# Rotated queries and keys stored to DRAM head by head instead of part by part

## The chip, the cores and the metric

The kernel runs on one core of one Trainium2 chip. The metric is device time in microseconds, here called us: the median over executions of the whole program, lower is better. A core has TensorE (PE, with its weight loads PEld), VectorE (DVE), ScalarE (ACT), GpSimd (POOL) and SyncE (SP). Each runs its own list of instructions in order. SyncE and GpSimd issue the DMA transfers, and sixteen transfer engines that they share carry them out.

## What is computed

The reference is one step of a two-layer decoder trunk for 1024 prompt tokens and 64 sample tokens that share weights. Layer 0 is attention with a window of 128 tokens, 16 query heads and 4 key heads of 64 dimensions; layer 1 is retention. The change lies in layer 0, where queries and keys are projected, rotated and used block by block:

```
q, k, v, g = split(h @ w_in)
q = rope(q);  k = rope(k)          # [x1*cos - x2*sin, x2*cos + x1*sin], two halves of 32
s = q @ k_band.T / 8               # 128 queries against this block's keys and the block's before
p = sink_softmax(s, sink, mask)
y = (p @ v_band * silu(g)) @ w_out
```

## The kernel before, in words

Tokens lie along the free dimension, 1088 of them in three chunks of 384, 384 and 320 (`CH`); the last 64 are the sample tokens. Every float32 product is made of three passes on values split into a high and a low part (`split`, L302 to L304: ScalarE writes the high part, VectorE the rest).

A projection of two weight slots is `pair_t` (its matmuls are L137 to L139). The columns of q and k are sorted so that the 128 partitions of a result are four heads of 32 rows, and the two results of a pair are the two halves of the rotary dimension. `attn_k` (L437) makes all four key heads at once; `attn_q` (L506) makes the four query heads of one key head `kv`, so there are four calls of it. For each chunk the evacuation scales and rotates the result on VectorE (`rope`), splits it into the tile `qk_hl` of shape [128 partitions = head and row, 2 = high or low, 2 = half, tokens], and stores it with four DMAs issued on GpSimd's queue: L448 for keys into `s_k`, L515 for queries into `s_q`. Each takes one part (high or low of one half), 128 partitions with one row of 384 tokens each, 1536 bytes (256 tokens, 1024 bytes, in the last chunk). In DRAM `s_k` is [head, part, 64 rows, token], and `s_q` is [kv, 128 rows = four parts of 32, head, token]. There are 12 stores of keys and 48 of queries. `qk_hl` has two buffers.

The attention itself is cut into units: for each of four `kv` eight blocks of 128 prompt tokens and two groups of sample tokens. `attn_load` (L548) issues a unit's loads on SyncE's queue: `qst` from `s_q` (L552), two copies of `kwin` from `s_k` (L557, 64 partitions each) and `vst` (L559). `attn_scores` multiplies them (L594, L595); softmax, transposes (`attn_turn`, L631, L654 to L658) and values (`attn_values`, L668, L682, L690) follow, and the gated result `og` goes to `s_og` by a store on GpSimd's queue (L693). `og` and `qst` have two buffers. Units run staggered and are woven into the stream of the remaining projections (`weave` in `layer0`): the matmuls of `L0_ORDER` (g0 q1 q2 g1 q3 g2 g3 and the two embedding projections p0 p1) give the beat, and steps of units are put between them at a fixed rate, once the chunk they need is in `self.done`. Weights come through SyncE's queue too (`wraw`, L109), as do the embeddings `praw` (L323), which are split into buffers of `qk_hl`.

The build plans each engine's order of instructions with a simulated time line (`schedule_with_timeline_sim=True`); which semaphore each waits for follows from what it reads and writes.

Of the kernel before, what the change touches and what calls it, by code (L numbers as in the profile page):

```python
# [9 lines left out]
F32 = mybir.dt.float32  # L10
# [45 lines left out]
class Trunk:  # L56
# [380 lines left out]
    def attn_k(self, pool, acts):  # L437
        nc = self.nc

        def evac(c, ps, c0, n):  # L440
            self.norm_rows(c)
            r = self.rope(pool, ps, n, c0)
            m = min(n, TP - c0)
            hl = pool.tile([P, 2, 2, 384], F32R, name="qk_hl")
            self.split(hl[:, 0, :, :m], hl[:, 1, :, :m], r[:, :, :m])
            for ab in range(2):
                for half in range(2):
                    nc.gpsimd.dma_start(self.s_k[:, ab, half * 32:half * 32 + 32, c0:c0 + m], hl[:, ab, half, :m].bitcast(F32))  # L448
            if c == 2:
                for half in range(2):  # L450
                    nc.gpsimd.dma_start(self.s_kn[half * 32:(half + 1) * 32, :, :].rearrange("r k t -> k r t"),
                                      r[:, half, 256:320])
                for lo, rows, dst in ((128, P, "p"), (256, TS, "s")):
                    pt = self.pa.tile([P, 512], F32, name="pa")
                    for half in range(2):
                        nc.tensor.transpose(pt[:rows, half * P:(half + 1) * P], r[:, half, lo:lo + rows], self.ident)
                    kn = pool.tile([P, 4, 2, 32], F32, name="knat" + dst, bufs=1)
                    nc.scalar.copy(kn[:rows], pt[:rows, 0:256].rearrange("p (h k r) -> p k h r", h=2, k=4))
                    flat = kn[:rows].rearrange("p k h r -> p (k h r)")
                    if dst == "p":  # L460
                        nc.gpsimd.dma_start(self.io["kwp"], flat)
                    else:
                        nc.gpsimd.dma_start(self.io["kws"][:, 120:128, :], flat)

        yield from self.pair_t(acts, evac)
# [40 lines left out]
    def attn_q(self, pool, acts, kv):  # L506
        nc = self.nc

        def evac_q(c, ps, c0, n):
            r = self.rope(pool, ps, n, c0)  # L510
            m = min(n, TP - c0)
            hl = pool.tile([P, 2, 2, 384], F32R, name="qk_hl")
            self.split(hl[:, 0, :, :m], hl[:, 1, :, :m], r[:, :, :m])
            for j in range(4):
                nc.gpsimd.dma_start(self.s_q[kv, j * 32:(j + 1) * 32, :, c0:c0 + m].rearrange("r h t -> h r t"),  # L515
                                  hl[:, j // 2, j % 2, :m].bitcast(F32))
            if c == 2:
                for half in range(2):
                    nc.gpsimd.dma_start(self.s_qs[kv, half * 32:(half + 1) * 32].rearrange("r h t -> h r t"),
                                      r[:, half, 256:320])  # L520
            self.done.add(("q", kv, c))

        yield from self.pair_t(acts, evac_q)
# [861 lines left out]
```

## Time and profile before

| what | us |
|---|---|
| median of 3 runs | 1669.41 |
| lowest and highest | 1668.7, 1670.39 |
| profiled execution, its own time | 1670.7 |
| its span, first to last instruction | 1668.9 |
| TensorE busy in the span | 1642.2 |
| mean granted TensorE clock | 0.997 |

The profile shows the one profiled execution; its times count from the span's start. Layer 0 with the changed stores takes the first quarter, to about 424 us. [...] A wait is put down to the releaser that came last by the profile.

### The profile page before, as it was taken

The page shows a single profiled execution, that of the slowest core. Times are in us where ns is not written, and L with a number is a line of the kernel's source. Part 1 is how long each engine was busy: PE and PEld are TensorE (multiplying, and loading weights), DVE is VectorE, ACT ScalarE, POOL GpSimd, SP SyncE. Part 2 cuts the span into 40 slices and gives each one's busy share as a digit, 9 for nine tenths or more (in the row PEclk, how much of TensorE's full clock was granted, in tenths as well). Part 3 has the DMA queues.
Part 4 walks back from the last instruction along what each step waited for, and adds up shares of the span by engine and source line. Part 5 has one row for each costly group of instructions (what it writes and reads, how often), then busy time and mean ns, then how long its engine had stood idle before and what let it go on. Part 6 is the DMA issues. An engine that isn't in the chain of part 4 may idle for free.

```text
span 1668.9 us, 26266 instructions
## 1 busy us (share of the span) xinstructions
PE 1642.2 (98%) x9656; PEld 1536.3 (92%) x9656; DVE 994.8 (60%) x1952; ACT 592.9 (36%) x1357; POOL 377.1 (23%) x610
## 2 busy tenths in 40 slices
PE   8999999999999999999999999999999999999998
PEld 7999898999999999799979998799978998999998
DVE  7569787977148585146734665456735765543952
ACT  6245454686334351222222312222222533231421
POOL 1515544345001121111122212131122221200000
PEclk9999999999999999999999999999999999999999
DMA  8655646586314443253545555365544766572342
GB/s 284 186 155 136 169 117 166 177 260 206 122 38 158 144 142 126 75 185 130 186 147 177 191 171 171 117 198 177 191 154 146 259 209 203 189 240 84 124 145 88
DMA packets 180175, 273.07 MB, mean 164 GB/s; under 512 B 30560, under 2 KB 129824, under 8 KB 180016
## 3 DMA queue, kind: packets, MB, share of 16 engines
q1 hardware_dynamic: 143216, 178.01, 34.8%
q0 software_dynamic: 36832, 93.40, 16.4%
q8 instruction: 76, 1.25, 0.3%
q14 instruction: 51, 0.42, 0.1%
HBM read 173.51 MB, written 99.68 MB: 164 GB/s over the span
## 4 chain that ended last, share of the span: by engine, by line
PE 71%; issue 2%; DMA 1%; POOL 0%; ACT 0%; DVE 0%; POOLq 0%; ACTq 0%; SPq 0%; DVEq 0%
PE pj L137 16%; PE pj L139 16%; PE pj L138 16%; PE pj L237 4%; PE pj L238 4%; PE pj L239 4%; PE pa L1109 1%; PE pa L1117 1%; PE pa L1042 1%; PE pa L984 1%; PE pa L1044 1%; PE pa L1043 1%; PE pa L953 1%; PE pa L1026 1%; PE pa L1025 1%
## 5 line engine op out<-in xcount | busy, mean ns | idle before, releaser
L137 PE MATMUL pj<-act,whi 128*128 128x384 f32 (+1 forms) x2160 | 711.7, 330 | 4.1 <-ACT ys L767 2.8
L139 PE MATMUL pj<-act,wlo 128*128 128x384 f32 (+1 forms) x2160 | 708.5, 328 | 0.0
L138 PE MATMUL pj<-act,whi 128*128 128x384 f32 (+1 forms) x2160 | 708.2, 328 | 0.0
L137 PEld LDWEIGHTS pj<-act,whi 128*128 128x128 f32 x2160 | 407.0, 188 | 10.2 <-ACT ys L767 3.1
L138 PEld LDWEIGHTS pj<-act,whi 128*128 128x128 f32 x2160 | 407.2, 189 | 3.2
L139 PEld LDWEIGHTS pj<-act,wlo 128*128 128x128 f32 x2160 | 406.9, 188 | 2.9 <-issue 0.8
L303 ACT CAST whi<-wraw 128x512 fp32r<-128x512 f32 (+1 forms) x226 | 128.0, 614 | 182.7 <-PE pj L138 130.0
L304 DVE TENSOR_TENSOR wlo<-wraw,whi 128x512 fp32r<-128x512 f32 (+1 forms) x226 | 146.3, 680 | 75.2 <-ACT whi L303 74.2
L237 PE MATMUL pj<-whi,act 128*128 128x512 f32 x256 | 102.4, 401 | 0.0
L238 PE MATMUL pj<-wlo,act 128*128 128x512 f32 x256 | 101.1, 395 | 0.0
L239 PE MATMUL pj<-whi,act 128*128 128x512 f32 x256 | 100.6, 394 | 0.0
L911 ACT ACTIVATE rp_a<-pj,rcol 128x512 f32<-128x512 f32 x32 | 22.0, 689 | 125.1 <-PE pj L239 97.6
L1119 DVE SCALAR_TENSOR_TENSOR s<-s,pa 128x512 f32<-128x512 f32 x64 | 42.7, 683 | 37.6 <-PE pa L1117 37.3
L352 DVE TENSOR_TENSOR rp_a<-pj,cs 128x768 f32<-128x768 f32 (+1 forms) x39 | 35.5, 911 | 49.4 <-PE pj L139 49.3
L542 ACT ACTIVATE s_sb<-s_sb,nm 128x129 f32<-128x129 f32 (+1 forms) x136 | 53.6, 397 | 30.8 <-DVE nm L539 30.5
L237 PEld LDWEIGHTS pj<-whi,act 128*128 128x128 f32 x256 | 48.1, 188 | 16.3 <-issue 3.4
L239 PEld LDWEIGHTS pj<-whi,act 128*128 128x128 f32 x256 | 48.1, 188 | 11.1
L238 PEld LDWEIGHTS pj<-wlo,act 128*128 128x128 f32 x256 | 48.1, 188 | 10.2
L1120 POOL DMA_DIRECT2D srs<-s x64 | 35.6, 557 | 92.8 <-DVE s L1119 90.7
L943 POOL TENSOR_TENSOR br<-bv,mhalf 128x1 f32<-128x1 f32 x36 | 29.5, 820 | 112.2 <-DVE bv L940 112.2
L840 DVE SCALAR_TENSOR_TENSOR ple_st<-ple_st,pleh 128x768 f32<-128x768 f32 (+2 forms) x25 | 22.0, 881 | 52.6 <-ACT ple_st L839 52.6
L364 ACT ACTIVATE rp_a<-rp_b 128x768 f32<-128x768 f32 (+1 forms) x36 | 29.2, 810 | 68.1 <-DVE rp_b L362 55.8
(252 smaller groups left out, 2580.9 us busy)
## 6 DMA issues: line engine op xcount, KB each, us to landing
wraw<-wt SPq DMA_DIRECT2D x110, 512.0 KB, 4.1
s<-st SPq DMA_DIRECT2D x16, 1024.0 KB, 6.5
srs<-s POOLq DMA_DIRECT2D x64, 256.0 KB, 2.9
act<-s_og SPq DMA_DIRECT2D x48, 192.0 KB, 3.7
qst<-s_q SPq DMA_DIRECT2D x32, 256.0 KB, 4.2
qk<-s_qk SPq DMA_DIRECT2D x32, 256.0 KB, 3.7
s_v<-rp_a POOLq DMA_DIRECT2D x32, 256.0 KB, 2.3
vl<-s_v SPq DMA_DIRECT2D x32, 256.0 KB, 2.8
```

The lines of the kernel that those rows point to most:

```text
L137: mm(ps, hi[:, sl], a[c][:, 0], start=start and i == 0, stop=False)
L138: mm(ps, hi[:, sl], a[c][:, 1], start=False, stop=False)
L139: mm(ps, lo[:, sl], a[c][:, 0], start=False, stop=stop and i == last)
L237: mm(o, hi, w[0][:, sl], start=first, stop=False)
L238: mm(o, hi, w[1][:, sl], start=False, stop=False)
L239: mm(o, lo, w[0][:, sl], start=False, stop=last)
L303: self.nc.scalar.copy(hi, x)
L304: self.nc.vector.tensor_tensor(out=lo, in0=x, in1=hi.bitcast(F32), op=ALU.subtract)
L352: nc.vector.tensor_tensor(out=ta, in0=ps, in1=self.cs[:, 0:1, c0:c0 + n].broadcast_to([P, 2, n]), op=ALU.mult)
L542: nc.scalar.activation(s[:, h, :], s[:, h, :], AF.Exp, bias=nm[:, h, :], scale=0.125, accum_out=den[:, h:h + 1])
L1119: nc.vector.scalar_tensor_tensor(out=s0, in0=s0, scalar=float(gam ** 8), in1=pd, op0=ALU.mult, op1=ALU.add)
L1120: nc.gpsimd.dma_start(self.io["srs"][4 * g + j, h, k * P:(k + 1) * P, :], s0)
```

## The change

The four stores of a chunk no longer take one part each for all heads. Each takes one head: 32 partitions, and from each of them all four parts, four rows of 384 tokens. On the DRAM side the same bytes go to the same places; the order of the dimensions in the access is now row, part, token, where it was head, row, token. The loads, the tiles and everything else stay.

```diff
@@ attn_k, evac
-            for ab in range(2):
-                for half in range(2):
-                    nc.gpsimd.dma_start(self.s_k[:, ab, half * 32:half * 32 + 32, c0:c0 + m], hl[:, ab, half, :m].bitcast(F32))
+            for k in range(4):
+                nc.gpsimd.dma_start(self.s_k[k, :, :, c0:c0 + m].rearrange("a (f r) t -> r (a f) t", f=2),
+                                    hl[k * 32:k * 32 + 32, :, :, :m].bitcast(F32).rearrange("r a f t -> r (a f) t"))
@@ attn_q, evac_q
-            for j in range(4):
-                nc.gpsimd.dma_start(self.s_q[kv, j * 32:(j + 1) * 32, :, c0:c0 + m].rearrange("r h t -> h r t"),
-                                  hl[:, j // 2, j % 2, :m].bitcast(F32))
+            for h in range(4):
+                nc.gpsimd.dma_start(self.s_q[kv, :, h, c0:c0 + m].rearrange("(j r) t -> r j t", j=4),
+                                    hl[h * 32:h * 32 + 32, :, :, :m].bitcast(F32).rearrange("r a f t -> r (a f) t"))
```

## Rows read from the trace of the kernel before

**Rows 1.** The page, busy us, share of the span and instructions of each engine.

```profile
PE 1642.2 (98%) x9656; PEld 1536.3 (92%) x9656; DVE 994.8 (60%) x1952; ACT 592.9 (36%) x1357; POOL 377.1 (23%) x610
```

**Rows 2.** What TensorE waited for: us in total, times, longest us.

```profile
PE pa L594 <- DMA wraw<-wt: 3.4, 1, 3.4
PE pa L682 <- ACT pts L658: 3.1, 1, 3.1
...
PE pa L668 <- ACT pth L303: 2.5, 1, 2.5
```

**Rows 3.** Stretches: length, busy us by engine, granted clock, DMA share, GB/s.

```profile
97.00:107.00 10.00, 6.63 (x32) 6.34 (x32) 4.15 (x8) 2.50 (x9) 0.10 (x1) 0.83 0.75 232
...
184.00:200.00 16.00, 12.91 (x83) 12.44 (x82) 9.57 (x22) 10.11 (x39) 5.44 (x8) 0.89 0.61 145
...
281.00:296.00 15.00, 12.50 (x72) 11.82 (x71) 9.02 (x18) 10.11 (x31) 1.09 (x4) 0.89 0.57 159
```

**Rows 4.** Time line of TensorE: start, us, instruction, idle before and releaser.

```profile
101.22 0.30 PE L594 MATMUL pa<-kwin,qst 128*128 128x128 f32 x1 [3.37 <-DMA wraw<-wt]
```

**Rows 5.** Time line of SyncE's queue: the first two loads of queries.

```profile
88.60 3.14 SPq L552 DMA_DIRECT2D qst<-s_q  x2
```

**Rows 6.** DMAs issued from 88 to 92 us: count, KB each, us to landing.

```profile
qst<-s_q SPq DMA_DIRECT2D x2, 256.0 KB, 12.2
...
s_q<-qk_hl POOLq DMA_DIRECT2D x2, 192.0 KB, 11.9
```

**Rows 7.** What SyncE's queue waited for, 74 to 92 us.

```profile
SPq L552 <- DMA s_q<-qk_hl: 13.7, 1, 13.7
```

**Rows 8.** Time line of GpSimd: stores of chunk 0 and chunk 1.

```profile
78.28 2.74 POOL L515 DMA_DIRECT2D s_q<-qk_hl  x4 [3.49 <-ACT qk_hl L303]
86.60 2.83 POOL L515 DMA_DIRECT2D s_q<-qk_hl  x4 [5.58 <-ACT qk_hl L303]
```

**Rows 9.** DMAs issued from 80.3 to 81 us, chunk 0's last stores.

```profile
s_q<-qk_hl POOLq DMA_DIRECT2D x2, 192.0 KB, 8.4
```

**Rows 10.** Time line of ScalarE before TensorE's second wait.

```profile
188.72 0.53 ACT L690 COPY og<-pa 64x32 f32<-64x32 f32 x4 [8.54 <-DMA s_og<-og]
```

**Rows 11.** DMAs issued from 178 to 178.7 us.

```profile
s_og<-og POOLq DMA_DIRECT2D x1, 128.0 KB, 10.6
```

**Rows 12.** All DMA issues of the span: count, KB each, median us to landing.

```profile
qst<-s_q SPq DMA_DIRECT2D x32, 256.0 KB, 4.2
...
kwin<-s_k SPq DMA_DIRECT2D x56, 128.0 KB, 4.3
s_q<-qk_hl POOLq DMA_DIRECT2D x32, 192.0 KB, 8.6
...
s_og<-og POOLq DMA_DIRECT2D x32, 128.0 KB, 3.4
...
s_x<-ys POOLq DMA_DIRECT2D x16, 192.0 KB, 2.8
...
s_v<-v_hl POOLq DMA_DIRECT2D x8, 256.0 KB, 3.8
...
praw<-pT SPq DMA_DIRECT2D x4, 384.0 KB, 5.4
```

**Rows 13.** Time line of ScalarE before TensorE's third wait.

```profile
283.14 0.83 ACT L303 CAST qk_hl<-praw 128x768 fp32r<-128x768 f32 x1 [4.18 <-DMA praw<-pT]
```

**Rows 14.** DMAs issued from 272 to 276 us.

```profile
praw<-pT SPq DMA_DIRECT2D x1, 384.0 KB, 7.6
```

**Rows 15.** Line 486, stores with four rows from each partition: ns min/median/max.

```profile
L486 POOL DMA_DIRECT2D s_v<-v_hl x8: 750/752/946, 35.0 to 46.1; - x8
```

**Rows 16.** Stretches of 2 us, columns as in rows 3.

```profile
80.00:82.00 2.00, 2.00 (x14) 2.00 (x13) 0.00 (x0) 0.00 (x0) 1.02 (x2) 1.00 0.28 44
...
84.00:86.00 2.00, 2.00 (x16) 2.00 (x15) 1.36 (x3) 0.53 (x1) 0.00 (x0) 1.00 0.47 120
...
100.00:102.00 2.00, 0.78 (x7) 0.81 (x8) 0.11 (x1) 0.00 (x0) 0.00 (x0) 1.00 0.98 354
```

## The prediction, made before the changed kernel ran

> **What bounds the kernel now.** I read the page's busy times first. TensorE is busy for 98% of the span [rows 1]: a change to stores can only win what TensorE idles, and what the lower clock after an idle stretch costs. So the second view is what TensorE waited for [rows 2]. Three of its waits lie in the attention stage, where the changed stores are: 3.4, 3.1 and 2.5 us. The third view shows the stretches around them [rows 3], and the reader is to see the granted clock beside the busy time: a mean of 0.83 over 10 us, 0.89 over 16 us and 0.89 over 15 us, while it is 1.00 elsewhere in the stage. [...] The lost time is (1 - clock) x stretch: 1.7, 1.8 and 1.65 us. One stop thus costs its wait and its clock: 3.37 + 1.7 = 5.1 us, 3.09 + 1.8 = 4.9 us, 2.5 + 1.65 = 4.15 us; 14.1 us together.
>
> Then I ask of each whether a changed store stands behind it.
>
> Stop 1. TensorE comes to the first scores of unit 0 at 101.22 - 3.37 = 97.85 us and starts them at 101.22 [rows 4]. The row names a weight load, but the matmul reads qst and kwin, and qst is what came last: SyncE issued its load at 88.60 [rows 5], and it took 12.2 us to land [rows 6], at 100.8. Why so late? SyncE had stood still for 13.7 us until the stores of s_q had landed [rows 7]; those four were issued from 78.28 at 0.69 us each [rows 8], and the last took 8.4 us to land [rows 9], so 80.3 + 8.4 = 88.7. And why 12.2 us for the load? It ran beside the next chunk's four stores, issued at 86.60 [rows 8], which themselves took up to 11.9 us [rows 6].
>
> Stop 2. TensorE waited for pts, which ScalarE wrote late because it stood for 8.5 us before og, until 188.7 [rows 10]: the buffer was still being stored. That store was issued on GpSimd's queue straight behind four stores of s_q and took 10.6 us to land [rows 11], against 3.4 us as a rule [rows 12].
>
> Stop 3. ScalarE stood 4.2 us for praw [rows 13], whose load took 7.6 us [rows 14]; four stores of s_q had been issued just before it.
>
> **The change, part by part.** Count and bytes stay: 48 stores of s_q and 12 of s_k, four to a chunk, 192 KB each [rows 12] and 128 in the last chunk by the code, every row still 1536 bytes (1024 in the last chunk). What changes is the shape of a store: 32 partitions with four rows each, instead of four groups (one per head) of 32 partitions with one row each, heads outermost.
>
> Issue on GpSimd: a store with four rows per partition is in the trace already, s_v: 0.75 us against 0.69 for s_q [rows 15]. 60 x 0.06 = 3.6 us more on GpSimd in the stage, 0.24 us per chunk, covered by GpSimd's idle time (it is busy 5.4 of the 16 us around stop 2, 1.1 of the 15 around stop 3 [rows 3]). If that cover were gone, the s_og store behind would start 0.24 us later, a tenth of the slack below. I put it at nothing.
>
> Landing: the changed store is not in the trace, so I bound it. Lower end: the fastest other stores of this size, s_x with 192 KB in 2.8 us [rows 12]. Upper end: no better, 8.4 us, or worse (rival 3). I take 3.8 us, from s_v [rows 12]: the row is nearest in what changes, partitions outermost and four rows apart within each, its rows 512 bytes in place of 1536 and its bytes more (256 KB); what it lacks is the narrowness, 128 partitions against 32. That the present form is slow for its shape and not for its bytes is what the fine windows say: with nearly only these stores in flight the transfer engines are busy to 0.28, at 44 GB/s, and later to 0.47, at 120, while a backlog a little later moves 354 GB/s at 0.98 [rows 16]. Most of the sixteen stand idle while everybody waits.
>
> [...]
>
> What then becomes of the stops. Stop 1: the last store of chunk 0 lands at 80.3 + 3.8 = 84.1 instead of 88.7. The qst load is issued 4.5 us earlier, before chunk 1's stores start at 86.6, and at its usual 4.2 us [rows 12] it lands at 88.3, 9 us before TensorE asks. Even a store of 7 us and a load of 8 us would do (80.3 + 7 + 8 = 95.3). The stop goes: 5.1 us. What is late next there is the load for unit 2, which needs unit 0's buffer; it follows unit 0's scores as before, only 3.4 us earlier, and TensorE does not wait for it now [rows 2].
>
> Stop 2: ScalarE went on to og, and then to pts, at 188.7; for TensorE not to wait the s_og store has to land 3.1 us earlier, in 7.5 us instead of 10.6. With the four stores ahead at 3.8 us it should need 3.4 to 5. It goes: 4.9 us. Stop 3: praw would have to land in 5.1 us instead of 7.6; its usual is 5.4 [rows 12], and a weight load competes too. It is open, and I count nothing for it.
>
> For s_k nothing is to be gained on TensorE: no wait of its own in [rows 2] lies where those loads are used first. A store by head also means that the first kwin loads need only the store of their own head; that too shortens a wait that costs nothing.
>
> Sum: 5.1 + 4.9 = 10.0 us off the profiled execution's 1670.7 us (span 1668.9), 1660.7. The median of the runs shown, 1669.41, is 1.3 below that execution, so the forecast is 1659.4 us.
>
> **The rivals.** (1) All three stops go. For it: the same stores stand beside the praw load. Against: 2.5 us are needed and the load's own median leaves 2.2. Time: 1669.4 - 14.1 = 1655.3.
>
> (2) The burst is bound by what the four stores move together, not by the form of each. 4 x 192 KB = 786 KB at the 120 GB/s of the best window with nearly only them in flight (84 to 86 us [rows 16]) take 6.6 us; with about 2.5 us of lead (at 80 to 82 us the rate is still 44 GB/s) they land at 87.4, 1.3 us sooner than now. Chunk 1 then still meets the qst load, and each stop shrinks by about 1 us: 1669.4 - 3 = 1666.4 at best and no change at worst. Against it: s_v stores of 256 KB follow each other closely too and land in 3.8.
>
> (3) Slower: the narrow source is the limit. Each store now draws on 32 partitions. If the last of a chunk then needs 12 us instead of 8.4, SyncE issues qst 3.6 us later, stop 1 grows by 3.6, and stop 2 by as much through the s_og store in the same queue: 1669.4 + 7.2 = 1676.6. It decides from the point where a chunk's last store needs more than 8.4 us. For it: kwin's loads to 64 partitions take 4.3 us for 128 KB where qst's to 128 take 4.2 for twice the bytes [rows 12]. Against: at 786 KB in 10 us the present rate is far under what the queues reach [rows 16].
>
> [...] No row of this trace shows a store of 32 partitions.
>
> (4) Part of the gain is taken back. The order of instructions on each engine is written by a planner at build time, from its own prices of transfers; other shapes may shift that order, and a new wait of 2 to 5 us with its clock may stand where TensorE runs ahead. One such stop leaves 1664 to 1668. The rows speak neither for nor against it.
>
> **How the numbers follow.** No change means within 0.2%, 3.3 us, about what a measurement of this kernel can tell. Forecast (stops 1 and 2 go, 3 stays or shrinks) 0.42; rival 1 0.20; rival 2 0.14; rival 3 0.10; rival 4 0.14. Faster: the forecast, rival 1 and most of rival 4, 0.72; no change: rival 2 and the rest of 4, 0.18; slower 0.10. The range runs from rival 1 with 1.3 us of small waits besides, 1654, to rival 2 at its worst, 1669.5; it leaves out rival 3 and a few per cent more. The forecast's own range is 1656 to 1663.
>
> **What would show it.** Right: s_q landing near 4 us instead of 8.6; SyncE's wait for s_q a few us instead of 13.7; no wait of TensorE before the first scores; granted clock 1.00 from 97 to 107 us; the s_og store behind a burst in about 4 us; ScalarE's wait before og gone. Rival 2 shows as first stores that land sooner and last ones that do not; rival 3 as landings above 8.4 us; rival 4 as a wait of TensorE at a line not in [rows 2]. The prediction is wrong if s_q lands in 4 us and the first stop stays: then qst was not what TensorE waited for.

## The result and the profile after

| | before | after |
|---|---|---|
| median, us | 1670.41 (6 runs, 1668.7 to 1676.4) | 1656.56 (6 runs, 1654.23 to 1658.56) |
| profiled execution, its own time | 1670.7 | 1655.34 |
| its span | 1668.9 | 1653.6 |
| mean granted clock | 0.997 | 0.999 |

The ratio is 0.9914, with a 95% interval of 0.9901 to 0.9927: faster by 0.9%, 13.9 us by the medians. The forecast was 1659.4, in a range of 1654.0 to 1669.5; it counted from a median before of 1669.41 (three runs), where six runs give 1670.41.

The page's busy line and what TensorE waited for in the kernel after, to be read beside [rows 1] and [rows 2]:

```profile
PE 1637.7 (99%) x9656; PEld 1532.7 (93%) x9656; DVE 995.0 (60%) x1952; ACT 593.8 (36%) x1357; POOL 371.8 (22%) x610
```

```profile
PE pa L196 <- ACT act L299: 5.0, 1, 5.0
PE pa L668 <- DVE pth L304: 1.4, 1, 1.4
PE pa L196 <- ACT whi L303: 1.1, 1, 1.1
```

The three stops of the attention stage are gone; the longest wait left, 5.0 us, lies at the program's start and was there before. A small one is new, 1.4 us at L668. The reader will miss a fourth line, which the prediction left out because it lies at the end of the layer. From what TensorE waited for in the kernel before:

```profile
PE pj L137 <- ACT ys L767: 2.8, 1, 2.8
```

The same three stretches as in [rows 3], shifted to where the work now stands, and one around the new wait (length, busy us by engine, granted clock, DMA share, GB/s):

```profile
94.00:104.00 10.00, 10.00 (x65) 10.00 (x64) 4.69 (x10) 3.45 (x12) 2.22 (x4) 1.00 0.51 145
...
180.00:196.00 16.00, 16.00 (x107) 15.44 (x106) 12.70 (x27) 10.41 (x39) 7.44 (x13) 1.00 0.82 221
...
276.00:292.00 16.00, 16.00 (x103) 15.59 (x102) 15.41 (x29) 10.40 (x26) 5.22 (x9) 1.00 0.60 178
...
360.00:370.00 10.00, 8.50 (x40) 7.25 (x39) 9.78 (x25) 6.52 (x23) 3.88 (x9) 0.83 0.65 218
```

TensorE is busy throughout the first three and the clock stays at 1.00; around the new wait the clock falls to 0.83. That gives an account of the 15.3 us between the two spans. Idle time of TensorE fell from 1668.9 - 1642.2 = 26.7 us to 1653.6 - 1637.7 = 15.9, by 10.8: the three stops 9.0, the wait for ys 2.8, less the new 1.4, and some tenths. Busy time fell by 4.5: the clock gave back 5.15 at the three stops and took 1.7 at the new wait, 3.45 net. Some 1 us has no row of its own. The profile's page gives the granted clock as a share of full speed: behind the first stop of the kernel before it reads 0.52 from 102 to 105 us, where matmuls of 384 columns start 0.32 us apart, and 1.00 from 108 to 111 us, where they start 0.17 to 0.18 us apart.

The DMA issues of the whole span, the answer to [rows 12]; then the first query loads in SyncE's time line and the stores in GpSimd's, for [rows 5] and [rows 8]:

```profile
qst<-s_q SPq DMA_DIRECT2D x32, 256.0 KB, 3.4
...
kwin<-s_k SPq DMA_DIRECT2D x56, 128.0 KB, 3.4
s_q<-qk_hl POOLq DMA_DIRECT2D x32, 192.0 KB, 3.8
...
s_og<-og POOLq DMA_DIRECT2D x32, 128.0 KB, 2.9
...
praw<-pT SPq DMA_DIRECT2D x4, 384.0 KB, 3.8
```

```profile
84.01 1.22 SPq L552 DMA_DIRECT2D qst<-s_q  x2
```

```profile
78.63 2.18 POOL L515 DMA_DIRECT2D s_q<-qk_hl  x4 [4.45 <-DVE qk_hl L304]
86.94 2.18 POOL L515 DMA_DIRECT2D s_q<-qk_hl  x4 [6.13 <-DVE qk_hl L304]
```

The 192 KB store lands in 3.8 us instead of 8.6, the loads beside it got quicker too, and qst is issued at 84.0 instead of 88.6.

### The profile page after: what moved, and what is told of

The parts are those of the page before. It is cut to its first block, busy times and chain, and to the rows that moved or that the text cites. A ratio compares the mean times of both kernels' runs of the same rounds, so it can differ in the third digit from the quotient of the medians.

```text
span 1653.6 us, 26261 instructions
## 1 busy us (share of the span) xinstructions
PE 1637.7 (99%) x9656; PEld 1532.7 (93%) x9656; DVE 995.0 (60%) x1952; ACT 593.8 (36%) x1357; POOL 371.8 (22%) x610
## 3 DMA queue, kind: packets, MB, share of 16 engines
q0 software_dynamic: 29792, 93.31, 15.7%
## 4 chain that ended last, share of the span: by engine, by line
PE 93%; DMA 2%; issue 2%; DVE 1%; ACT 1%; POOL 0%; SPq 0%; POOLq 0%; DVEq 0%; ACTq 0%
PE pj L137 22%; PE pj L139 22%; PE pj L138 22%; PE pj L237 4%; PE pj L238 4%; PE pj L239 4%; PE pa L1109 1%; PE pa L1117 1%; PE pa L1042 1%; PE pa L984 1%; PE pa L1044 1%; PE pa L1043 1%; PE pa L953 1%; PE pa L595 1%; PE pa L594 1%
## 5 line engine op out<-in xcount | busy, mean ns | idle before, releaser
L238 PEld LDWEIGHTS pj<-wlo,act 128*128 128x128 f32 x256 | 48.1, 188 | 10.2
L362 DVE TENSOR_TENSOR rp_b<-pj,rbc 128x768 f32<-128x768 f32 (+1 forms) x36 | 32.7, 909 | 34.8 <-PE pj L139 34.8
```

Of the source, the lines that this page charges most:

```text
L238: mm(o, hi, w[1][:, sl], start=False, stop=False)
```

## Experiments

A cause named in advance had to be told from others: that the landing of the query stores decides (my theory); that it is the planner's order of instructions, which did change (TensorE's list of instructions differs from the one before in several hundred places); that it is the keys; that it is not the outermost size but something else about the store. Every ratio below is to the kernel before, run on the same chip.

**e1: each kind of store alone.** Added to the changed kernel behind its last output, with a vector instruction that rewrites the tile between the steps, so that each waits for the one before; `d2` is [2, 65, 4, TP] and `d8` [8, 17, 4, TP], so that the outer dimension cannot be merged. After the five single stores come four by part, four by head, four wide, and the four small ones:

```diff
+part = lambda d, j: g(d[j * 32:(j + 1) * 32, :, 0:384].rearrange("r h t -> h r t"), x[:, j // 2, j % 2, :])
+head = lambda d, h: g(d[:, h, 0:384].rearrange("(j r) t -> r j t", j=4),
+                      x[h * 32:h * 32 + 32].rearrange("r a f t -> r (a f) t"))
+wide = lambda d, j: g(d[:, 0, 0:384], x[:, j // 2, j % 2, :])
...
+    for h in range(4):
+        g(ds[0:32, h, 0:384], x[h * 32:h * 32 + 32, 0, 0, :])
...
+             lambda: g(d2[:, 0:64, 0, 0:384], x[:, 0, 0, :]), lambda: g(d8[:, 0:16, 0, 0:384], x[:, 0, 0, :]),
```

> The changed kernel with a tail: after its last output is computed, stores of one tile go to scratch memory of their own, each kind alone with nothing else issued beside it. One store by part (four heads outermost), one by head (32 partitions, four rows each), one wide (the same 128 rows as by part, but as one dimension of 128), one with 2 and one with 8 outermost; then four by part, four by head, four wide, and four small ones (32 partitions, one row each). Spread theory (the outermost size decides): by part 5 to 6 us to landing, 2 outermost 7 or more, 8 outermost 3 to 4, wide and by head 2.3 to 2.8; the last of four by part about 8, of four by head and four wide 3 to 4; small 2 to 2.5. Packet theory (the 6 KB that lie together in a partition of the by-head store decide): wide, 2 and 8 outermost take the 5 to 6 us of by part, only by head is quick. Narrow theory (32 partitions cost something): by head is slower than wide by 0.5 us or more. The time of the whole grows by the tail, some 60 us, and says nothing.

DMA issues of the tail, one row from a window around each step (count, KB each, median us to landing); below them the last store of each burst of four 192 KB stores, from a window around that one:

```profile
d_part<-prb POOLq DMA_DIRECT2D x1, 192.0 KB, 5.4
d_head<-prb POOLq DMA_DIRECT2D x1, 192.0 KB, 2.6
d_wide<-prb POOLq DMA_DIRECT2D x1, 192.0 KB, 2.2
d_two<-prb POOLq DMA_DIRECT2D x1, 192.0 KB, 7.5
d_eight<-prb POOLq DMA_DIRECT2D x1, 192.0 KB, 3.7
...
d_small<-prb POOLq DMA_DIRECT2D x4, 48.0 KB, 1.8
...
d_part<-prb POOLq DMA_DIRECT2D x1, 192.0 KB, 8.2
d_head<-prb POOLq DMA_DIRECT2D x1, 192.0 KB, 3.7
d_wide<-prb POOLq DMA_DIRECT2D x1, 192.0 KB, 2.6
```

Two, four, eight and 128 outermost: 7.5, 5.4, 3.7, 2.2 us for the same rows of the same tile. The wide store has exactly the rows of the store by part and is the quickest of all, so neither the length of a row nor what lies together in a partition explains the slow form; the outermost size does. What passes between size and time stands in the packet records of e1's trace (start, length and size of each packet). All of a store's 196608 bytes go in 44 to 48 packets of 1536 to 4608 bytes. With 2, 4 and 8 outermost and wide, a packet of 4608 bytes takes about as long in each case, 178, 178, 178 and 196 ns in the median; what differs is how many of these packets move at once, and that number stands longest at 2, 4, 8 and 16. By head it stands longest at 16 too. Why the outermost size sets that number is not shown: the records do not name the engines.

The narrow theory holds in small: by head is 0.4 us slower than wide alone, just under the 0.5 us named in advance, and 1.1 us at the end of a burst. With as many packets in flight, one of 4608 bytes takes 361 ns in the median by head and 196 wide. What makes a packet slower by head is not shown. The price is far below the 3.6 us that rival 3 would have needed.

**e2 and e3: keys alone, queries alone.** e2 takes the first hunk of the change, e3 the second.

> Only the 12 stores of keys go by head, those of queries by part as before; the planner writes TensorE's order as in the kernel before. My theory (the query stores make the stops): ratio 1.000 to the kernel before, within 0.2%, the waits of 3.4, 3.1 and 2.5 us stay. Rival (the keys, which come first and free SyncE's queue, start the gain): faster by 5 us, 0.997, with the first stop gone.

> Only the 48 stores of queries go by head; every engine's order is that of the changed kernel. My theory: the whole gain, 0.991 to 0.993, no wait of TensorE over 1.5 us in the attention stage. Rival (the keys bring part of it): 0.994 to 0.997, with one of the stops back.

e2: ratio 0.9989 (0.9972 to 1.0005). What TensorE waited for in e2:

```profile
PE pa L682 <- ACT pts L658: 4.0, 1, 4.0
PE pa L594 <- DMA wraw<-wt: 3.3, 1, 3.3
PE pj L137 <- ACT ys L767: 2.8, 1, 2.8
```

The keys land in 4.2 us and SyncE waits only 3.9 us for the first of them, and still TensorE's first two stops stand. The third does not show in this execution, although the query stores were not changed: the load of praw landed in 5.3 us here and ScalarE waited 1.9 us for it. That stop was the least settled of the three. e3: ratio 0.9915 (0.9892 to 0.9938), the whole gain, with keys that land in 7.6 us (7.7 in the kernel before). The rival of the keys falls.

**e4: only the first query group by part again.**

```diff
+            if kv == 0:
+                for j in range(4):
+                    nc.gpsimd.dma_start(self.s_q[kv, j * 32:(j + 1) * 32, :, c0:c0 + m].rearrange("r h t -> h r t"),
+                                      hl[:, j // 2, j % 2, :m].bitcast(F32))
+            else:
...
```

> The changed kernel, with the stores of the first query group (kv 0) by part again. My theory: the first stop returns, 3.4 us before the first scores and some 1.7 us of clock, with qst again the load that comes last, and no other: 0.994 to 0.995 to the kernel before. Rival (the planner's other order took the stops away, whichever way the stores go): no wait before the first scores, 0.991 to 0.992.

Built this way the orders of TensorE, ScalarE, VectorE and SyncE are those of the changed kernel. The first scores in TensorE's time line, and two stretches around them:

```profile
101.56 0.30 PE L599 MATMUL pa<-kwin,qst 128*128 128x128 f32 x1 [3.45 <-DMA wraw<-wt]
```

```profile
98.00:104.00 6.00, 2.55 (x16) 2.48 (x16) 2.68 (x5) 0.84 (x1) 0.00 (x0) 0.93 0.73 240
104.00:110.00 6.00, 6.00 (x32) 6.00 (x31) 2.02 (x6) 2.59 (x11) 0.00 (x0) 0.79 0.34 98
```

(L599 is L594 of the kernel before.) The stop is back at 3.45 us, with a clock loss of 0.07 x 6 + 0.21 x 6 = 1.7 us; the qst load, issued at 88.4 beside the next burst, took 13.2 us to land, until 101.6, when TensorE starts. Nothing but twelve stores differs. The ratio, 0.9933 (0.991 to 0.9957), lies between what my theory and the rival expected and its interval holds both: the trace tells them apart, the ratio does not. In the profiled execution the wait at L668 brought no clock loss (its stretch stays at 1.00). One execution of the five took 1654.6 us, as little as the changed kernel's; what TensorE waited for in it is not recorded.

**e5: a third buffer for og in the kernel before.**

```diff
-        og = pool.tile([P, 2, P], F32, name="og", bufs=2)
+        og = pool.tile([P, 2, P], F32, name="og", bufs=3)
```

> The kernel before, all stores by part, with a third buffer for og; TensorE's and SyncE's orders are those of the kernel before. My theory of the second stop (ScalarE stands before og because its buffer is still being stored, behind a slow burst in GpSimd's queue): ScalarE's wait before og and TensorE's 3.1 us before L682 go, the first stop stays at 3.4; ratio 0.997, some 5 us. Rival (the values of that unit are late for another reason, its pts or loads): the wait at L682 stays at 2 us or more, ratio 0.999 to 1.001.

Ratio 0.9963 (0.9947 to 0.9978). What TensorE waited for:

```profile
PE pa L594 <- DMA kwin<-s_k: 5.0, 1, 5.0
PE pa L196 <- ACT act L299: 4.9, 1, 4.9
PE pj L137 <- ACT ys L767: 2.9, 1, 2.9
PE pa L668 <- ACT pth L303: 1.3, 1, 1.3
```

The wait at L682 is gone with stores by part and TensorE's old order: the second stop was the buffer of og, held by a store that landed late. The first stop stays (5.0 us here, put down to another load).

**e6 and e7: without the planner.** `schedule_with_timeline_sim=False` in the kernel before and in the changed one; TensorE's lists then differ in 60 lines only, but ScalarE's and VectorE's still differ in about 300 and 270.

> The kernel before without the planner: every engine takes its instructions in the order in which the program names them. Base for the next run. Both theories: the query stores land in 7 to 9 us, and some waits of TensorE in the attention stage are there; the time may be anywhere from 1660 to 1720.

> The changed kernel without the planner, so that its order differs from the run before in few places (60 lines of TensorE's 8,900) and the form of the stores is the difference. My theory: faster than the run before by what TensorE's waits on late query stores cost there, 5 to 15 us. Rival (the planner's order made the gain): the two within 3 us of each other.

e6: 1703.41 us, ratio 1.0182 (1.0152 to 1.0212), query stores of 192 KB land in 10.2 us. e7: 1692.31 us, 1.0120 (1.0098 to 1.0142), 3.7 us. The difference is 11.1 us of medians with nearly one order of TensorE. TensorE's waits in the attention stage differ most at the attention's values:

```profile
PE pa L668 <- ACT pth L303: 3.8, 1, 3.8
...
PE pa L668 <- DVE ptm L648: 2.5, 3, 1.6
...
PE pa L668 <- DVE og L674: 1.5, 1, 1.5
PE pa L594 <- DVE s_sb L602: 1.5, 1, 1.5
```

These are e6's; in e7 the first is 0.5, the second 1.7, and the last two are gone. The form by head is worth about as much in another order, at other waits; how much of the 11.1 us is due to the orders of ScalarE and VectorE is not separated.

**e8, e9, e10: stores by part on 128 partitions, made wide.** The scratch tensors are laid out so that the 128 rows of a store are one dimension; qst is loaded in two DMAs.

```diff
-        self.s_q = scratch("s_q", [4, P, 4, TP])
+        self.s_q = scratch("s_q", [4, 2, P, 2, TP])
+            for ab in range(2):
+                for half in range(2):
+                    nc.gpsimd.dma_start(self.s_q[kv, ab, :, half, c0:c0 + m], hl[:, ab, half, :m].bitcast(F32))
+            for a in range(2):
+                src = self.s_q[kv, a, :, :, n * P:(n + 1) * P].rearrange("(h r) f t -> (r f) h t", h=4)
+                nc.sync.dma_start(u["q"][a * 64:a * 64 + 64].bitcast(F32), src)
```

> All stores by part again, but the scratch tensors laid out so that the 128 rows of a store are one dimension of 128; queries are loaded by two DMAs of 64 partitions instead of one of 128. My theory: stores land in 2.3 to 2.8 us, a little sooner than by head, and the time is that of the changed kernel within 0.2% (0.990 to 0.993 to the kernel before), since no wait of TensorE is left for them to shorten. Rival (every us of landing counts): 0.988 or less. Rival (the form by part is itself at fault): landing above 5 us and 0.997 or more.

> The changed kernel once more, beside the wide one on the same chip, to tell 0.1% apart. Ratio 0.990 to 0.993 to the kernel before.

> The wide stores once more. My theory (a sooner landing is worth nothing where no wait of TensorE hangs on it): within 0.15% of the changed kernel in the run before. Rival (the 1.1 us that a burst lands sooner are worth something): 0.2% or more below it.

e8: 0.9898 (0.9876 to 0.9919), query stores of 192 KB in 2.8 us: by part is as quick as any once its outermost dimension is 128. Side by side on one chip, e9 (by head) has 1657.59 us, 0.9912 (0.9897 to 0.9926), and e10 (wide) 1654.13 us, 0.9895 (0.988 to 0.9911). The medians differ by 3.5 us, 0.21%, the ratios by 0.17%, and the intervals overlap; by the one the rival is met, by the other it is between the two, and it stays open. In e10 TensorE does not wait at L668, where e9 waits 1.4 us. Its order differs from the changed kernel's in many lines, so even a real gain would not be the landing's alone.

**e11 and e12: one group by part, in two orders.** e11 takes group 3 back to by part, e12 group 2, with the condition of e4.

> The changed kernel with the stores of the last query group (kv 3) by part. The planner then writes TensorE's order as in the kernel before but for 35 lines, while the stores of groups 0 to 2 go by head. My theory (late landings make the stops, in either order): the first stop and the one before L682 are gone; the third, behind a load of praw beside group 3's stores, may return with 1 to 2.5 us, and the wait of 2.8 us for ys at the end of the layer returns with the order; ratio 0.993 to 0.996. Rival (the order makes the stops): all of 3.4, 3.1 and 2.8 us are back, 0.998 to 1.001.

> The changed kernel with the stores of query group 2 by part, in the changed kernel's order but for 23 lines of TensorE's. My theory of the second stop: the s_og store behind that burst again takes 7 us or more to land, ScalarE again stands 4 us or more before og, TensorE 2 to 4 us before L682; the first scores do not wait; ratio 0.993 to 0.996. Rival (the second stop was bound to the old order): no wait at L682, 0.990 to 0.993.

e11: 0.9929 (0.9912 to 0.9946), at the edge of the 0.993 to 0.996 expected. TensorE's waits from 50 to 420 us, and the stretch of the first scores:

```profile
PE pj L137 <- ACT ys L767: 3.0, 1, 3.0
PE pj L137 <- ACT rp_a L342: 1.2, 1, 1.2
PE pa L668 <- ACT s_sb L601: 0.7, 1, 0.7
```

```profile
94.00:104.00 10.00, 10.00 (x65) 10.00 (x64) 4.67 (x10) 3.04 (x11) 2.64 (x5) 1.00 0.56 162
```

With nearly the old order the first two stops are gone because groups 0 to 2 land early, ScalarE waits 2.8 us for praw again, until 270.7, but TensorE only 0.7, at 281.0 (the 1.2 us lie at 357), and the wait for ys is back. The first two stops follow the landings; the wait for ys follows the order. The third stop follows ScalarE's wait for praw, run by run: 4.2, 3.4, 2.8 and 1.9 us in the kernel before, e5, e11 and e2, and TensorE's longest wait at L668 near it is 2.5, 1.3, 0.7 and none.

e12: 0.9908 (0.989 to 0.9926), no loss beside e9's 0.9912 on the same chip. The s_og store behind group 2's burst, and what ScalarE and TensorE did about it, from 150 to 200 us:

```profile
s_og<-og POOLq DMA_DIRECT2D x1, 128.0 KB, 9.4
```

```profile
ACT og L690 <- DMA s_og<-og: 5.9, 1, 5.9
```

```profile
PE pa L631 <- ACT og L690: 1.5, 1, 1.5
```

The mechanism returns as in [rows 10] and [rows 11], 9.4 us and 5.9 us, but TensorE loses only 1.5, without loss of clock over the 16 us around it. I had expected 2 to 4, before L682. I had also expected a ratio of 0.993 to 0.996; no wait at L682 and 0.990 to 0.993 is what the rival had named. So the late store and ScalarE's wait come back in this order, but the second stop at its full price shows only in the old one. Why the order lets so little of ScalarE's wait through is not shown.

## Why the prediction was right, point by point

*Stop 1.* Right in each link: store 3.8 us, as I had estimated from s_v's row (in e1 2.6 us alone and 3.7 as the last of four), qst issued at 84.0 (84.1 was forecast), no wait, clock 1.00. e4 shows the price: 3.45 + 1.7 us, in one order of instructions.

*Stop 2.* Right: s_og behind the burst lands in 4.8 us in the kernel after (3.4 to 5 was forecast), and ScalarE no longer waits there. e5 shows the link through og's buffer by itself. Its price of 4.9 us holds for the old order; in the new one, e12 shows 1.5 us for the same late store.

*Stop 3.* I counted nothing for it and gave its going 0.20 as rival 1. It went: praw's load behind the last burst lands in 3.7 us instead of 7.6. Its 4.15 us are a little more than the 3.9 us by which the measured gain, 13.9, exceeds the 10.0 forecast, and 1656.56 lies nearer to rival 1's 1655.3 than to 1659.4. What I mis-sized is the load: I took its usual 5.4 us [rows 12] as what remains. That median is of three loads that behave differently, 7.6 behind the burst, 3.5, and 5.4 some 90 us after the last query store, beside other stores; in the kernel after they take 3.7, 3.9 and 3.8. How far the load's time was the burst's doing is not shown by a run of its own.

*What was not in the sum.* The wait for ys, 2.8 us, which I left out as lying outside the stage, and the new wait at L668 with 1.4 us and up to 1.7 of clock. That they nearly cancel is luck. Both hang on the planner's order, which is rival 4's mechanism: the first stands also in e2, e5 and e11, in or near the old order, the second also in e3, e4, e9 and e12, in or near the new one. By terms, all read from the two profiled executions: 14.1 + 2.8 - 3.1 = 13.8, beside 15.3 between their spans; the 13.9 of the medians is another measure, and that it agrees so closely says little.

*Rival 2* (the burst is bound by what moves together): in e1 the last of four stores by head lands in 3.7 us against 2.6 for one alone, so four cost 1.1 us more, where the rival needed 87.4 - 80.3 = 7 us for the last. *Rival 3* (narrow): real, at 0.4 to 1.1 us.

*Issue on GpSimd.* Forecast 0.75 us, from s_v; it is 0.55, less than the 0.69 by part. Hidden either way.

*A sign read wrongly.* I wrote that SyncE would wait for s_q "a few us" instead of 13.7. It waits 10.2: it comes to that point at 73.8, while the stores are not issued until 78.6. My own figures, 13.7 - 4.5 = 9.2, said so.

## What to carry to other kernels

For a DMA like these stores, whose partition dimension has to be split into (outer, inner) on the DRAM side, look at the outer size first: with 2, 4, 8 and 128 the same 192 KB landed in 7.5, 5.4, 3.7 and 2.2 us. Choose the tile's cut or the scratch tensor's layout so that the outermost dimension is large: in the kernel, 32 by head landed in 3.8 us and 128 in e8 in 2.8, where 4 took 8.6. A store is worth hurrying only if something waits behind it (in e2 the keys landed in 4.2 us instead of 7.7, at a ratio of 0.9989): look for the buffer it holds, the load that reads it back, and the loads that run beside it. When a stop of TensorE goes, count the clock it cost as well, and read it from the stretch behind that stop, since it is not the same for every wait: 1.65 us behind the 2.5 us at L668 of the kernel before, none behind its 2.8 us for ys.

## What was not expected of the hardware

Packets. The DMA packets that the trace counts around each store of e1 hold 192 KB in each case, but by the line of packet sizes 324 packets under 512 bytes with 2 outermost, 150 with 4 (by part), 64 with 8, and 16 by head and wide. The line of the store by part, then of the one by head:

```profile
DMA packets 194, 0.20 MB, mean 39 GB/s; under 512 B 150, under 2 KB 150, under 8 KB 194
```

```profile
DMA packets 64, 0.20 MB, mean 73 GB/s; under 512 B 16, under 2 KB 16, under 8 KB 64
```

Over the whole program the software queue moved 36832 packets before and 29792 after, 7040 fewer in 60 stores. The packet records of e1 settle what the small packets are worth: each holds 4 to 12 bytes and takes 9 ns in the median, and the 148 of the store by part itself (two more in its window belong to another queue) take 1.3 us in sum where its 44 data packets take 12.2. They go with the slow form and do not make its time.

The clock's price of a short wait is not fixed either. The same 1.4 us at L668 cost 1.7 us of clock in the profile of the kernel after, and none in another execution of the same kernel, e9's (granted clock 1.00 from 360 to 372 us around it), nor in e4's. In the kernel before, the wait for ys, 2.8 us, cost none (1.00 from 420 to 440 us), while the 2.5 us at L668 cost 1.65.
